# Two 256-column matmuls for one of 512, and 320 bytes of small tiles packed so that operand buffers swap their places modulo 256 bytes

## The chip, the cores and the metric

The kernel runs on one core of one Trainium2 chip. The metric is device time in microseconds (us), from the program's start to its end. The profile used here is one profiled execution on that core: its span, from the first to the last recorded instruction, is 1807.0 us. The timed runs are separate executions. TensorE does the matmuls, VectorE (DVE), ScalarE (ACT) and GpSimd (POOL) the elementwise work, SyncE (SP) issues nearly all transfers.

## What is computed

A trunk of two layers is applied to two groups of 512 tokens with a model width of 1024, in float32. Layer 0 is differential attention, layer 1 a retention in both directions, and a final RMSNorm closes the trunk.

```python
def diff_attention(h, w_in, ...):
    proj = h @ w_in                              # (512, 1024) @ (1024, 8192)
    q, k, v, gate = jnp.split(proj, ...)
    ...                                          # rotary q, k; 8 heads, two softmaxes each
    a = p[:, :, 0] - lam * p[:, :, 1]
    o = einsum('bhqk,bkhe->bqhe', a, v)
    o = rms_norm(o, subln_g, SUBLN_EPS) * (1.0 - lambda_init)
    return (o * silu(gate)) @ w_out              # (512, 2048) @ (2048, 1024)

def bidir_retention(h, w_in, ...):
    proj = h @ w_in                              # (512, 1024) @ (1024, 6144)
    ...                                          # rotated q, k; decayed scores in chunks, both directions
    return (rms_norm(o_f + o_b) * silu(gate)) @ w_out

def trunk(x, ...):
    x = x + diff_attention(rms_norm(x, norm_g[0]), ...)
    x = x + bidir_retention(rms_norm(x, norm_g[1]), ...)
    return rms_norm(x, final_norm_g, NORM_EPS)
```

The two input projections, the two output projections and the attention products are where TensorE's time goes.

## The kernel before

**Precision.** Each float32 operand is split in a high and a low part of the matmul's own float32 format, and a product is the sum of three passes, high by high, high by low and low by high (`PASSES`). ACT writes the high part (`hi_of`, L400), DVE the low one (`lo_of`, L403).

**Projections.** An input projection is cut into units of 256 output columns, and both token groups and both halves of the contraction are combined as in Strassen's scheme in Winograd's form: seven products P1 to P7 per unit instead of eight. The token side of a product is one of seven operands B11, B21, T1, T2, B22, T3, T4, each four tiles of 128 x 2 x 512 (high and low parts), which stay in memory for the whole layer. The weight side is combined, split and put into a ring of seven buffers called `ws`. There are two kinds of units:

- In a *pair* unit (`pair`, L596 to L601: q, k and the gates) the weights are the stationary operand, 128 x 128, and the token operand is the moving one, 512 columns wide. A product is four parts of the contraction by three passes: 12 matmuls into one bank of PSUM. All of them are recorded on L599.
- In a *wide* unit (`wide`, L603 to L612: v) it is the other way round: the token operand is stationary, the weights are the moving one, 256 columns wide, and a product is 48 matmuls into halves of two banks. They are recorded on L609.

Both write the same PSUM ring tiles `pj`, `sc` and `o`. The matmul that opens a bank has `start` set, and where a bank is filled by halves only the first of the two has it.

**The other matmuls.** Attention scores are on L1116 (512 columns), attention times values on L1181 (256), transposes on L1161, L815, L1028 and L716, the retention on L1315, L1339, L1359 and L1367 (256), and the output projection on L891 (512), where the head's output is stationary and the weights in `ws` move.

**Order.** Every operation is given to a planner with a cost and its dependences; `arrange` lays the operations of all five engines out in one simulated order and the kernel issues them in it. A pair product has the cost 2.79 there, whatever it consists of. Instructions of one engine run in the issued order.

**Memory.** Four pools follow each other in every partition of the on-chip memory: `sm` (small tiles of a few elements, each taking 32 bytes), `cp` (large buffers `b`, the identity and tables), `ar` (one tile `arena`, cut into slots of 4 KB that begin 128 bytes in, some of them shifted by 64 or 128 bytes), and `wk` (the rings `ws`, `raw`, `st`, `os`, `c`, `e`, `m`). All large tiles are multiples of 512 bytes, so that the bytes of `sm` and the padding of `arena` set where everything behind them begins modulo 256:

| | large buffers in cp | unshifted slots of the arena | slots shifted by 64 and 128 | rings |
|---|---|---|---|---|
| before | 32 | 32 | 96, 160 | 224 |

The small tiles that the change touches are the column of -0.5 (`mhalf`, 4 elements) and of -1.0 (`minus1`), the twelve one-element tiles of the ring `ssf`, and the two tiles `ls` and `neglam` of the attention's lambda.

Of the kernel before, what the change touches and what calls it, by code (L numbers as in the profile page):

```python
# [19 lines left out]
NT = S // P  # L20
NH = 8
# [5 lines left out]
LAMBDA_INIT = 0.8 - 0.6 * math.exp(-0.3 * 0)  # L27
# [226 lines left out]
def trunk_kernel(  # L254
# [7 lines left out]
    nc = tc.nc  # L262
# [14 lines left out]
    places = {}  # L277
    cnt = [0]

    def view(pool, tag, i, size, shape, dt=F32):  # L280


        if size % 16 and pool in (cp, wk):
            pool = sm
        if (tag, i) not in places:
            places[tag, i] = pool.tile([P, size], F32, tag=f"{tag}{i}", name=f"{tag}_{i}", bufs=1)
        n = math.prod(shape[1:])
        t = places[tag, i][0:shape[0], 0:n]
# [9 lines left out]
        size = SIZE.get(tag, shape[1])  # L298
        return Buf(plan, tag, bufs, lambda i: view(wk, tag, i, size, shape, dt))

    arena = ar.tile([P, 18 * 1024 + 80], F32R, tag="arena", name="arena")

    def slot(n, shape, dt=F32R, shift=0):

# [19 lines left out]
    def const(shape, tag, dt=F32, size=None):  # L324
        return Buf(plan, tag, 1, lambda i: view(cp, tag, i, size or math.prod(shape[1:]), shape, dt))
# [27 lines left out]
    def bank(tag, name=None):  # L353
        return Buf(plan, tag, BUFS[tag], lambda i: view(pj if tag == "pj" else sc, tag, i, S, [P, S]))
# [23 lines left out]
    def pool(n, fn, r, w):  # L378
        plan.op("POOL", 0.15 + 0.0024 * n, fn, r, w)
# [25 lines left out]

    ident = const([P, P], "ident")
    dma(lambda: ident.t, lambda: ident_in, [], [ident], 64, nc.scalar)
    mhalf = const([P, NT], "mhalf")
    dve(4, lambda: nc.vector.memset(mhalf.t, -0.5), [], [mhalf])
    minus1 = const([P, 1], "minus1")  # L410
    dve(1, lambda: nc.vector.memset(minus1.t, -1.0), [], [minus1])
    rows = work("m", [P, P], 4, name="rows")
    gcol = const([P, 28], "gcol")
    dve(1, lambda: nc.vector.memset(gcol[:, 20:21], D * EPS), [], [(gcol, 4)])
# [103 lines left out]
    class Unit:  # L518
# [67 lines left out]
        def product(self, op):  # L586
            which = BANK_OF[op]
            n_banks = 2 if self.wide else 1
            opens = op in OPENS
            if opens:  # L590
                self.banks[which] = [bank(self.tags[which], which) for _ in range(n_banks)]
            a, b = self.ops.pop(op), B_OF[op]
            bt = [Bop[b, k] for k in range(4)]
            reads = [q[1] for q in a] + bt

            def pair(ps, ks=range(4)):  # L596
                for k in ks:
                    for i, (u, v) in enumerate(PASSES):
                        nc.tensor.matmul(  # L599
                            ps.t, a[u][0]()[:, k, :], bt[k][:, v, :], start=(opens and k == 0 and i == 0),  # L600
                            stop=(k == 3 and i == 2), skip_group_check=True)  # L601

            def wide(ps, t):  # L603
                if self.led and op == "P1" and t == 0:
                    for j in range(NT):
                        nc.tensor.transpose(ps[:, j * P:(j + 1) * P], ident.t, ident.t)
                for k in range(4):
                    for i, (u, v) in enumerate(PASSES):
                        nc.tensor.matmul(  # L609
                            ps[:, (t % 2) * 256:(t % 2) * 256 + 256], bt[k][:, v, t * P:(t + 1) * P],  # L610
                            a[u][0]()[:, k, :], start=(opens and t % 2 == 0 and k == 0 and i == 0),
                            stop=(k == 3 and i == 2), skip_group_check=True)  # L612

            if not self.wide:
                ps = self.banks[which][0]
                if op == "P1" and self in first_units[:2]:
                    for k in range(4):
                        pe(0.7, lambda k=k: pair(ps, (k,)), reads[:2] + [bt[k]], [(ps, k)])
                else:
                    pe(2.79, lambda: pair(ps), reads, [ps])  # L620
                return
            for t in range(NT):
                ps = self.banks[which][t // 2]
                led = self.led and op == "P1" and t == 0
                pe(1.87 if led else 1.43, lambda ps=ps, t=t: wide(ps, t), reads + [ident] * led, [ps])
# [185 lines left out]
    def norm_cols(sq, ps, guard):  # L811

        def fn():
            for t in range(2):
                nc.tensor.transpose(ps[:, t * P:(t + 1) * P], sq[:, t * P:(t + 1) * P], ident.t)  # L815
        pe(0.22, fn, [sq, ident], [ps])
        ss, rr = col(2, "css"), col(2, "crr", 9)
        for t in range(2):
            act(P + 120, lambda t=t: nc.scalar.activation(
                ps[:, 256 + t * P:256 + (t + 1) * P], ps[:, t * P:(t + 1) * P], AF.Copy, accum_out=ss[:, t:t + 1]),  # L820
                [(ps, t)], [(ps, 2 + t), (ss, t)])
        guard(ss)
        pool(200, lambda: nc.gpsimd.tensor_tensor(rr.t, ss.t, mhalf[:, 0:2], op=ALU.pow), [ss, mhalf], [rr])
        return rr

    def new_oT(g):
# [94 lines left out]
    def row_norm(g, t):  # L921

        ss, r = halves.pop((g, t)), col(1, "rsf", 4)
        pool(200, lambda: nc.gpsimd.tensor_tensor(r.t, ss.t, mhalf[:, 0:1], op=ALU.pow), [ss, mhalf], [r])
        return r


# [84 lines left out]
    def x_norm(g, t, late=()):  # L1012
        ss, r = col(1, "ssf", 12), col(1, "rsf", 4)
        jk = slot(16 + t % 2, [P, D])
        x = xnat[g, t]
        act(1250, lambda: nc.scalar.activation(jk.t, x.t, AF.Square, accum_out=ss.t), [x, *late], [jk, ss])
        pool(60, lambda: nc.gpsimd.tensor_scalar(ss.t, ss.t, 1.0 / D, EPS, op0=ALU.mult, op1=ALU.add), [ss], [ss])
        pool(200, lambda: nc.gpsimd.tensor_tensor(r.t, ss.t, mhalf[:, 0:1], op=ALU.pow), [ss, mhalf], [r])
        evac(D, lambda: x.t, lambda: x.t, lambda: r.t, [x, r], [x], 0.00058)

    def x_source(layer, tiles, turn):
# [47 lines left out]
    lp = work("m", [P, 2, P], 4, name="lp")  # L1069
    for i in range(2):  # L1070
        dve(P, lambda i=i: nc.vector.tensor_tensor(
            lp[:, i, :], lv.t.rearrange("p a s -> p (a s)")[:, 2 * i * P:(2 * i + 1) * P],
            lv.t.rearrange("p a s -> p (a s)")[:, (2 * i + 1) * P:(2 * i + 2) * P], op=ALU.mult), [lv], [(lp, i)])
    ls, neglam, lr = const([P, 2], "ls"), const([P, 1], "neglam"), const([P, 2, NH], "lr")
    dve(256, lambda: nc.vector.tensor_reduce(ls.t, lp.t, op=ALU.add, axis=AX.X), [lp], [ls])
    act(2, lambda: nc.scalar.activation(ls.t, ls.t, AF.Exp), [ls], [ls])
    dve(2, lambda: nc.vector.tensor_tensor(neglam.t, ls[:, 1:2], ls[:, 0:1], op=ALU.subtract), [ls], [neglam])
    dve(2, lambda: nc.vector.tensor_scalar(neglam.t, neglam.t, -LAMBDA_INIT, None, op0=ALU.add), [neglam], [neglam])
    act(16, lambda: nc.scalar.activation(lr.t, dec.t, AF.Exp), [dec], [lr])
    dve(8, lambda: nc.vector.tensor_scalar(lr[:, 0, :], lr[:, 0, :], -1.0, None, op0=ALU.mult), [lr], [lr])  # L1080
    dma(lambda: powers.t, lambda: dist_in[:, D:].rearrange("p (h t) -> p h t", h=NH), [], [powers], 16)
    for i in range(2):
        dve(16, lambda i=i: nc.vector.tensor_tensor(
            powers[:, :, 2 * i:2 * i + 2], powers[:, :, 2 * i:2 * i + 2], lr[:, i, :].unsqueeze(2).broadcast_to([P, NH, 2]),
            op=ALU.mult), [lr, powers], [powers])
# [52 lines left out]
    def combine(i):  # L1138

        p, sm, n = st[i]['p'], st[i - i % 2]['sm'], i % 2  # L1140
        rc, cc = col(tag="rc"), col(tag="cc")
        on, eng = (pool, nc.gpsimd) if i >= NT else (dve, nc.vector)
        if i >= NT:
            pool(200, lambda: nc.gpsimd.tensor_tensor(rc.t, sm[:, 2 + n:3 + n], minus1.t, op=ALU.pow),
                 [(sm, (1, n)), minus1], [rc])
        else:
            dve(2, lambda: nc.vector.reciprocal(rc.t, sm[:, 2 + n:3 + n]), [(sm, (1, n))], [rc])
        on(100, lambda: eng.tensor_scalar(
            cc.t, sm[:, n:n + 1], rc.t, neglam.t, op0=ALU.mult, op1=ALU.mult), [(sm, (0, n)), rc, neglam], [cc])
# [303 lines left out]
    for i in range(N2 + 1):  # L1453
        if i < N2:
            b, c = chunks[i]
# [78 lines left out]
```

## Time and profile before

| | |
|---|---|
| time of the runs, median of 3 | 1810.51 us (1808.48 to 1814.37) |
| span of the profiled execution | 1807.0 us, 3.5 below that median |
| granted TensorE clock, mean | 0.999 |
| TensorE matmul busy | 1794.9 us, 99% |
| TensorE weight load busy | 1558.1 us, 86% |
| DVE, ACT, POOL busy | 1477.1, 895.1, 169.5 us |
| busy share of the 16 DMA engines in the 40 slices | 0.2 to 0.8 |

PE is the matmul side of TensorE and PEld its weight loads, which run beside the matmuls before them. Matmuls are pipelined: the duration recorded of one contains its way through the array, so that the time a matmul adds is not that duration but the distance from its start to the next one's. That distance is read from rows of the timeline and of the chain of waits that give a start and a count: for a run of n equal matmuls it is the next row's start less this row's, divided by n. In the timeline each row has start, duration, engine, line, operation and tiles; in a list of stretches each row has the stretch, its length, and each engine's busy time with the instructions in it.

### The profile page before, as it was taken

To read this page: it belongs to the slowest core of one execution; us is meant where nothing else is said; L and a number is where in the kernel's file an instruction comes from. 1 tells how busy PE (TensorE), PEld (TensorE's weight loads), DVE (VectorE), ACT (ScalarE), POOL (GpSimd) and SP (SyncE) were. 2 spreads that over 40 slices of the span, in tenths; PEclk is the share of its full clock that TensorE was granted. 3 is DMA by queue.
4 is the path that set the end of the run, shared out by engine and by line. 5 is a ranking of instruction groups with operands and counts; after the bars stand their busy time and mean duration, and the time that the engine had idled before them with its cause. 6 is when DMAs were issued, how large, how long until landed. Compare 5 with 4: busy or idle time off the path is not lost.

```text
span 1807.0 us, 27780 instructions
## 1 busy us (share of the span) xinstructions
PE 1794.9 (99%) x10299; PEld 1558.1 (86%) x10299; DVE 1477.1 (82%) x2319; ACT 895.1 (50%) x1856; POOL 169.5 (9%) x323
## 2 busy tenths in 40 slices
PE   9999999999999999999999999999999999999998
PEld 6789889898988888888888888898989898888887
DVE  7958787778699888888888897787887967888887
ACT  7753444433434565554555866444434355444346
POOL 1000000000000022222322300000000000111113
PEclk9999999999999999999999999999999999999999
DMA  6444455555545685444554524464657559765662
GB/s 217 134 126 137 161 140 178 184 168 155 174 126 175 201 334 198 178 156 159 190 204 140 190 73 146 140 210 146 205 156 228 151 170 396 272 238 182 225 218 94
DMA packets 162767, 328.81 MB, mean 182 GB/s; under 512 B 12724, under 2 KB 76872, under 8 KB 162632
## 3 DMA queue, kind: packets, MB, share of 16 engines
q1 hardware_dynamic: 162304, 326.71, 54.1%
q8 instruction: 81, 1.33, 0.3%
q14 instruction: 54, 0.44, 0.1%
q10 hardware_dynamic: 328, 0.34, 0.1%
HBM read 209.55 MB, written 117.44 MB: 181 GB/s over the span
## 4 chain that ended last, share of the span: by engine, by line
PE 93%; DVE 2%; DMA 2%; ACT 2%; issue 1%; POOL 0%; SPq 0%; POOLq 0%; DVEq 0%; ACTq 0%
PE pj L599 20%; PE pj L891 19%; PE sc L599 10%; PE pj L609 10%; PE o L599 8%; PE o L1181 5%; PE sc L1116 5%; PE sc L609 5%; PE o L609 2%; PE o L1359 2%; PE tp L1161 2%; PE sc L1315 1%; PE o L1367 1%; PE tp L1339 1%; DMA raw<-in_ret_w_out_dram 1%
## 5 line engine op out<-in xcount | busy, mean ns | idle before, releaser
L891 PE MATMUL pj<-ws,arena 128*128 128x512 f32 x1542 | 391.2, 397 | 0.0
L891 PEld LDWEIGHTS pj<-ws,arena 128*128 128x128 f32 x1542 | 277.7, 188 | 52.7
L599 PE MATMUL pj<-b,ws 128*128 128x512 f32 x1080 | 265.0, 392 | 0.0
L599 PEld LDWEIGHTS pj<-b,ws 128*128 128x128 f32 x1080 | 201.4, 188 | 43.0
L403 DVE TENSOR_TENSOR ws<-st,ws 128x512 fp32r<-128x512 f32 (+1 forms) x192 | 147.9, 774 | 74.8 <-ACT ws L400 56.7
L896 DVE SCALAR_TENSOR_TENSOR b<-pj,crr,b 128x512 f32<-128x512 f32 (+1 forms) x257 | 189.9, 744 | 21.4 <-PE pj L891 21.0
L403 DVE TENSOR_TENSOR ws<-raw,ws 128x512 fp32r<-128x512 f32 (+1 forms) x164 | 141.5, 868 | 71.3 <-ACT ws L400 61.0
L400 ACT CAST ws<-st 128x512 fp32r<-128x512 f32 (+1 forms) x192 | 132.4, 693 | 121.4 <-PE pj L599 36.4
L599 PE MATMUL sc<-arena,ws 128*128 128x512 f32 x768 | 186.8, 392 | 0.0
L599 PE MATMUL o<-arena,ws 128*128 128x512 f32 x744 | 180.0, 393 | 1.1 <-ACT m L385 0.6
L599 PEld LDWEIGHTS sc<-arena,ws 128*128 128x128 f32 x768 | 144.0, 188 | 31.3
L400 ACT CAST ws<-raw 128x512 fp32r<-128x512 f32 (+1 forms) x164 | 125.7, 772 | 87.0 <-PE o L599 45.0
L599 PEld LDWEIGHTS o<-arena,ws 128*128 128x128 f32 x744 | 138.4, 188 | 31.7 <-DVE arena L463 1.4
L599 PE MATMUL pj<-arena,ws 128*128 128x512 f32 x648 | 160.3, 392 | 0.4 <-DVE arena L463 0.4
L599 PEld LDWEIGHTS pj<-arena,ws 128*128 128x128 f32 x648 | 120.8, 188 | 26.7 <-DVE arena L463 0.7
L1134 ACT ACTIVATE b<-sc,nm 128x512 f32<-128x512 f32 x128 | 88.0, 689 | 66.9 <-DVE nm L1124 66.5
L636 ACT COPY c<-pj 128x512 f32<-128x512 f32 x104 | 60.9, 586 | 119.7 <-PE pj L599 66.4
L609 PE MATMUL pj<-ws,b 128*128 128x256 f32 x960 | 116.8, 276 | 0.0
L609 PEld LDWEIGHTS pj<-ws,b 128*128 128x128 f32 x960 | 113.2, 188 | 0.7
L1116 PE MATMUL sc<-arena 128*128 128x512 f32 x384 | 101.2, 395 | 0.3 <-ACT b L1134 0.3
L1181 PEld LDWEIGHTS o<-arena 128*128 128x128 f32 x768 | 93.1, 188 | 2.7
L1181 PE MATMUL o<-arena 128*128 128x256 f32 x768 | 93.7, 278 | 0.0
(207 smaller groups left out, 2855.9 us busy)
## 6 DMA issues: line engine op xcount, KB each, us to landing
qk<-os SPq DMA_DIRECT2D x192, 256.0 KB, 3.6
arena<-qk SPq DMA_DIRECT2D x96, 512.0 KB, 5.8
raw<-in_da_w_in_dram SPq DMA_DIRECT2D x64, 512.0 KB, 5.1
v<-os SPq DMA_DIRECT2D x64, 512.0 KB, 4.3
arena<-v SPq DMA_DIRECT2D x64, 512.0 KB, 4.1
raw<-in_ret_w_in_dram SPq DMA_DIRECT2D x48, 512.0 KB, 4.8
os<-g SPq DMA_DIRECT2D x32, 512.0 KB, 7.4
g<-e SPq DMA_DIRECT2D x48, 256.0 KB, 4.6
```

What stands on the lines that cost most here:

```text
L400: act(n, lambda: nc.scalar.copy(dst(), src()), r, w)
L403: dve(n, lambda: nc.vector.tensor_tensor(dst(), src(), hi().bitcast(F32), op=ALU.subtract), r, w)
L599: nc.tensor.matmul(ps.t, a[u][0]()[:, k, :], bt[k][:, v, :], start=(opens and k == 0 and i == 0), stop=(k == 3 and i == 2), skip_group_che ...
L609: nc.tensor.matmul(ps[:, (t % 2) * 256:(t % 2) * 256 + 256], bt[k][:, v, t * P:(t + 1) * P], a[u][0]()[:, k, :], start=(opens and t % 2 == ...
L636: act(S, lambda c=c, ps=ps: nc.scalar.copy(c.t, ps.t), [ps], [c])
L891: nc.tensor.matmul(ps[:, here], o[a][:, e, t * P:(t + 1) * P], u[b][:, e, here], start=(m == 0), stop=(m == 5))
L896: axpy(n, lambda half=half, here=here, ps=ps: nc.vector.scalar_tensor_tensor(half, ps[:, here], rr[:, t % 2:t % 2 + 1], half, op0=ALU.mult ...
L1116: nc.tensor.matmul(s.t, q[:, a, t * P:(t + 1) * P], k[:, b, :], start=(n == 0), stop=(n == 2))
L1134: act(840, lambda j=j, s=s, m=m: nc.scalar.activation(p[:, j, :], s.t, AF.Exp, bias=m.t, accum_out=sm[:, 2 * j + n:2 * j + n + 1]), [s, m] ...
L1161: nc.tensor.transpose(tp[:, j * P:(j + 1) * P], p[:, 0, j * P:(j + 1) * P], ident.t)
L1181: nc.tensor.matmul(o[:, e * 256:(e + 1) * 256], v[b][:, j, e * P:(e + 1) * P], aT[a][:, j, :], start=(n == 0), stop=(n % 12 == 11), skip_g ...
L1359: nc.tensor.matmul(o[:, e * 256:(e + 1) * 256], v_[v][:, 2 * c + j, e * P:(e + 1) * P], a_[:, u, j * 256:(j + 1) * 256], start=(e == 0 and ...
```

## The change

- `pair` issues two matmuls of 256 columns, left half and right half of the bank, with the same stationary operand one after the other, where there was one of 512. `start` is set for the left one of the first pass alone.
- `minus1` becomes a fifth column of `mhalf`, `neglam` a third column of `ls`, and the twelve tiles of `ssf` become columns of one tile of 32. `sm` is 320 bytes shorter by that (twelve times 32 less 128, and twice 32).
- `arena` is 32 elements (128 bytes) longer.

Behind that the buffers begin, modulo 256:

| | large buffers in cp | unshifted slots of the arena | slots shifted by 64 and 128 | rings |
|---|---|---|---|---|
| after | 224 | 224 | 32, 96 | 32 |

On each of the five engines the instructions stand in the same order as before, with two matmuls of 256 in the place of each one of 512 on L599.

```diff
+        if tag == "ssf":
+            if tag not in places:
+                places[tag] = sm.tile([P, 16 + 16], F32, tag=tag, name=tag, bufs=1)
+            return places[tag][:, i:i + 1]
...
-    arena = ar.tile([P, 18 * 1024 + 80], F32R, tag="arena", name="arena")
+    arena = ar.tile([P, 18 * 1024 + 112], F32R, tag="arena", name="arena")
...
-    mhalf = const([P, NT], "mhalf")
-    dve(4, lambda: nc.vector.memset(mhalf.t, -0.5), [], [mhalf])
-    minus1 = const([P, 1], "minus1")
-    dve(1, lambda: nc.vector.memset(minus1.t, -1.0), [], [minus1])
+    mhalf = const([P, NT + 1], "mhalf")
+    dve(4, lambda: nc.vector.memset(mhalf[:, 0:NT], -0.5), [], [(mhalf, 0)])
+    dve(1, lambda: nc.vector.memset(mhalf[:, NT:NT + 1], -1.0), [], [(mhalf, 1)])
...
             def pair(ps, ks=range(4)):
                 for k in ks:
                     for i, (u, v) in enumerate(PASSES):
-                        nc.tensor.matmul(
-                            ps.t, a[u][0]()[:, k, :], bt[k][:, v, :], start=(opens and k == 0 and i == 0),
-                            stop=(k == 3 and i == 2), skip_group_check=True)
+                        for c in range(2):
+                            here = slice(c * 256, (c + 1) * 256)
+                            nc.tensor.matmul(
+                                ps[:, here], a[u][0]()[:, k, :], bt[k][:, v, here],
+                                start=(opens and k == 0 and i == 0 and c == 0),
+                                stop=(k == 3 and i == 2), skip_group_check=True)
...
-    ls, neglam, lr = const([P, 2], "ls"), const([P, 1], "neglam"), const([P, 2, NH], "lr")
+    ls, lr = const([P, 3], "ls"), const([P, 2, NH], "lr")
...
-    dve(2, lambda: nc.vector.tensor_tensor(neglam.t, ls[:, 1:2], ls[:, 0:1], op=ALU.subtract), [ls], [neglam])
-    dve(2, lambda: nc.vector.tensor_scalar(neglam.t, neglam.t, -LAMBDA_INIT, None, op0=ALU.add), [neglam], [neglam])
+    dve(2, lambda: nc.vector.tensor_tensor(ls[:, 2:3], ls[:, 1:2], ls[:, 0:1], op=ALU.subtract), [(ls, 0)], [(ls, 1)])
+    dve(2, lambda: nc.vector.tensor_scalar(ls[:, 2:3], ls[:, 2:3], -LAMBDA_INIT, None, op0=ALU.add),
+        [(ls, 1)], [(ls, 1)])
```

The rest of the diff names the new columns where the old tiles were read.

More of the change, by code (lines that the diff above doesn't have):

```diff
@@ L822, in norm_cols @@
         guard(ss)
-        pool(200, lambda: nc.gpsimd.tensor_tensor(rr.t, ss.t, mhalf[:, 0:2], op=ALU.pow), [ss, mhalf], [rr])
+        pool(200, lambda: nc.gpsimd.tensor_tensor(rr.t, ss.t, mhalf[:, 0:2], op=ALU.pow), [ss, (mhalf, 0)], [rr])
         return rr
@@ L923, in row_norm @@
         ss, r = halves.pop((g, t)), col(1, "rsf", 4)
-        pool(200, lambda: nc.gpsimd.tensor_tensor(r.t, ss.t, mhalf[:, 0:1], op=ALU.pow), [ss, mhalf], [r])
+        pool(200, lambda: nc.gpsimd.tensor_tensor(r.t, ss.t, mhalf[:, 0:1], op=ALU.pow), [ss, (mhalf, 0)], [r])
         return r
@@ L1017, in x_norm @@
         pool(60, lambda: nc.gpsimd.tensor_scalar(ss.t, ss.t, 1.0 / D, EPS, op0=ALU.mult, op1=ALU.add), [ss], [ss])
-        pool(200, lambda: nc.gpsimd.tensor_tensor(r.t, ss.t, mhalf[:, 0:1], op=ALU.pow), [ss, mhalf], [r])
+        pool(200, lambda: nc.gpsimd.tensor_tensor(r.t, ss.t, mhalf[:, 0:1], op=ALU.pow), [ss, (mhalf, 0)], [r])
         evac(D, lambda: x.t, lambda: x.t, lambda: r.t, [x, r], [x], 0.00058)
@@ L1073, in trunk_kernel @@
             lv.t.rearrange("p a s -> p (a s)")[:, (2 * i + 1) * P:(2 * i + 2) * P], op=ALU.mult), [lv], [(lp, i)])
-    ls, neglam, lr = const([P, 2], "ls"), const([P, 1], "neglam"), const([P, 2, NH], "lr")
-    dve(256, lambda: nc.vector.tensor_reduce(ls.t, lp.t, op=ALU.add, axis=AX.X), [lp], [ls])
-    act(2, lambda: nc.scalar.activation(ls.t, ls.t, AF.Exp), [ls], [ls])
-    dve(2, lambda: nc.vector.tensor_tensor(neglam.t, ls[:, 1:2], ls[:, 0:1], op=ALU.subtract), [ls], [neglam])
-    dve(2, lambda: nc.vector.tensor_scalar(neglam.t, neglam.t, -LAMBDA_INIT, None, op0=ALU.add), [neglam], [neglam])
+    ls, lr = const([P, 3], "ls"), const([P, 2, NH], "lr")
+    dve(256, lambda: nc.vector.tensor_reduce(ls[:, 0:2], lp.t, op=ALU.add, axis=AX.X), [lp], [(ls, 0)])
+    act(2, lambda: nc.scalar.activation(ls[:, 0:2], ls[:, 0:2], AF.Exp), [(ls, 0)], [(ls, 0)])
+    dve(2, lambda: nc.vector.tensor_tensor(ls[:, 2:3], ls[:, 1:2], ls[:, 0:1], op=ALU.subtract), [(ls, 0)], [(ls, 1)])
+    dve(2, lambda: nc.vector.tensor_scalar(ls[:, 2:3], ls[:, 2:3], -LAMBDA_INIT, None, op0=ALU.add),
+        [(ls, 1)], [(ls, 1)])
     act(16, lambda: nc.scalar.activation(lr.t, dec.t, AF.Exp), [dec], [lr])
@@ L1143, in combine @@
         if i >= NT:
-            pool(200, lambda: nc.gpsimd.tensor_tensor(rc.t, sm[:, 2 + n:3 + n], minus1.t, op=ALU.pow),
-                 [(sm, (1, n)), minus1], [rc])
+            pool(200, lambda: nc.gpsimd.tensor_tensor(rc.t, sm[:, 2 + n:3 + n], mhalf[:, NT:NT + 1], op=ALU.pow),
+                 [(sm, (1, n)), (mhalf, 1)], [rc])
         else:
@@ L1148, in combine @@
         on(100, lambda: eng.tensor_scalar(
-            cc.t, sm[:, n:n + 1], rc.t, neglam.t, op0=ALU.mult, op1=ALU.mult), [(sm, (0, n)), rc, neglam], [cc])
+            cc.t, sm[:, n:n + 1], rc.t, ls[:, 2:3], op0=ALU.mult, op1=ALU.mult), [(sm, (0, n)), rc, (ls, 1)], [cc])
         axpy(S, lambda: nc.vector.scalar_tensor_tensor(
```

## Prediction

> **What bounds the kernel now.** I read the page's first part, then the chain that ended last, then the timeline of TensorE.
>
> ```profile
> PE 1794.9 (99%) x10299; PEld 1558.1 (86%) x10299; DVE 1477.1 (82%) x2319; ACT 895.1 (50%) x1856; POOL 169.5 (9%) x323
> PEclk9999999999999999999999999999999999999999
> PE 93%; DVE 2%; DMA 2%; ACT 2%; issue 1%; POOL 0%; SPq 0%; POOLq 0%; DVEq 0%; ACTq 0%
> ```
>
> The reader is to see that matmuls cover 99% of the span, at a clock that no slice shows throttled, and that 93% of the chain is matmul. So the time is the number of matmuls times the distance between their starts, and what other engines do counts only if they come to delay a matmul. DVE has 18% in hand over the span, so a PE that is half a per cent faster doesn't run into it.
>
> The change has two edits: one alters the number and width of the matmuls of L599, the other where operands begin. How many matmuls the first reaches:
>
> ```profile
> L599 PE MATMUL pj<-b,ws 128*128 128x512 f32 x1080 | 265.0, 392 | 0.0
> L599 PE MATMUL sc<-arena,ws 128*128 128x512 f32 x768 | 186.8, 392 | 0.0
> L599 PE MATMUL o<-arena,ws 128*128 128x512 f32 x744 | 180.0, 393 | 1.1 <-ACT m L385 0.6 <-DVE arena L463 0.3
> L599 PE MATMUL pj<-arena,ws 128*128 128x512 f32 x648 | 160.3, 392 | 0.4 <-DVE arena L463 0.4
> L599 PE MATMUL sc<-b,ws 128*128 128x512 f32 x120 | 29.1, 391 | 0.0
> ```
>
> That is 3360 matmuls, 280 products of 12.
>
> **What a matmul of either width costs.** The timeline (start, duration, engine, line, operation) and the chain (start, length, count):
>
> ```profile
> 163.42 5.63 PE L609 MATMUL o<-ws,arena 128*128 128x256 f32 x48
> 168.88 5.60 PE L609 MATMUL sc<-ws,arena 128*128 128x256 f32 x48
> 174.32 0.84 PE L609 MATMUL pj<-ws,b 128*128 128x256 f32 x6
> ...
> 190.64 1.54 PE L599 MATMUL pj<-arena,ws 128*128 128x512 f32 x6
> ```
>
> ```profile
> 210.01 8.24 PE pj L599 x36
> 218.25 2.75 PE o L599 x12
> ```
>
> Three pair products take 218.25 - 210.01 = 8.24 us, 2.747 us a product, 228.9 ns for a matmul of 512 columns. Wide units already run 256 columns with a fresh weight load each: 48 take 174.32 - 168.88 = 5.44 us, 113.3 ns each, and the whole stretch of 240 takes 190.64 - 163.42 = 27.22 us, 113.4 ns. Two of these are 226.7 ns. So 256-column matmuls are, in this trace, a little cheaper per column.
>
> **The split, step by step.** It adds 3360 matmuls and 3360 weight loads and leaves the columns the same. What carries the added loads:
>
> ```profile
> 163.42:190.64 27.22, 27.22 (x241) 27.22 (x240) 19.34 (x29) 12.07 (x20) 0.00 (x0) 1.00 0.56 172
> 486.38:626.46 140.08, 140.08 (x615) 114.93 (x614) 125.00 (x201) 59.54 (x105) 0.00 (x0) 1.00 0.50 153
> ```
>
> In a stretch of L609 the weight side is busy for all of the 27.22 us (third figure), in one of L599 for 114.93 of 140.08. The split moves L599 from the second regime to the first: a load no longer hides with room to spare under its matmul, it fills the distance. In the first regime nothing is left over, and yet 240 in a row held 113.4 ns.
>
> A product becomes 24 x 113.3 = 2.720 us instead of 2.747: -0.027 us, times 280 = -7.5 us. The first 48 of a run cost 168.88 - 163.42 = 5.46, 0.02 us more than settled ones; wide and pair units then have the same width, so what pair runs pay at their start, wide runs may save at theirs: I put 0.
>
> There is another spacing of 256-column matmuls, here called the long one, and the upper bound of the price comes from it:
>
> ```profile
> 705.64 1.64 PE L891 MATMUL pj<-ws,arena 128*128 128x512 f32 x6
> 707.12 2.99 PE L1181 MATMUL o<-arena 128*128 128x256 f32 x24
> 709.95 1.56 PE L1116 MATMUL sc<-arena 128*128 128x512 f32 x6
> ...
> 793.64 2.92 PE L1181 MATMUL o<-arena 128*128 128x256 f32 x24
> 796.39 0.60 PE L1161 MATMUL tp<-ident,b 128*128 128x128 f32 x4
> ```
>
> ```profile
> L1315 PE MATMUL sc<-arena 128*128 128x256 f32 x192 | 28.0, 282 | 0.1
> ```
>
> The same 24 matmuls of L1181 take 2.75 us at 793.64 and 2.83 at 707.12, 117.9 ns each. L1315 shows the same spacing as a mean: 282 ns recorded, where L609's rows below have 276 and 277. A pair product at the long spacing costs +0.083 us. So the split is worth between -7.5 and 280 x 0.083 = +23 us. I take -7.5: the nearest row is L609, whose moving and stationary operands begin at 224 and 32 modulo 256, exactly where the changed pair's do.
>
> **The new places.** Every address is still 32 modulo 64; what moves is the stationary operand's place less the moving one's, modulo 256. L599 goes from 224 - 32 = 192 to 32 - 224 = 64, L609 from 64 to 192, L891 (160 and 224 before, 96 and 32 after) from 192 to 64. Matmuls with both operands in the arena and large buffers keep theirs.
>
> - L609, 2688 matmuls, comes to 192. Rows of 256 columns at that relation are L1359 and L1367:
>
> ```profile
> 1560.46 1.52 PE L1359 MATMUL o<-arena 128*128 128x256 f32 x12
> 1561.82 0.84 PE L1367 MATMUL o<-arena,b 128*128 128x256 f32 x6
> 1562.50 1.55 PE L891 MATMUL pj<-ws,arena 128*128 128x512 f32 x6
> L609 PE MATMUL pj<-ws,b 128*128 128x256 f32 x960 | 116.8, 276 | 0.0
> L609 PE MATMUL sc<-ws,arena 128*128 128x256 f32 x768 | 89.6, 276 | 0.0
> L609 PE MATMUL pj<-ws,arena 128*128 128x256 f32 x576 | 73.1, 277 | 0.0
> L609 PE MATMUL o<-ws,arena 128*128 128x256 f32 x384 | 45.0, 277 | 0.0
> ```
>
> 1.36 / 12 and 0.68 / 6 are 113.3 ns too. Taken: 0; at worst all of it at the long spacing, 2688 x 4.6 = +12.4 us; at best the 0.02 at the head of its runs, under 1 us.
>
> - L891, 1530 matmuls, comes to 64, where no 512-column matmul of this trace stands. Its price now, from the chain, and its count:
>
> ```profile
> 1783.58 13.76 PE pj L891 x60
> L891 PE MATMUL pj<-ws,arena 128*128 128x512 f32 x1530 | 389.8, 398 | 0.0
> ```
>
> 13.76 / 60 = 229.3 ns. At twice the settled 256-column price it would gain 2.6 ns, -4.0 us in all; at twice the long one, 235.8, it would lose +9.9. Taken: 0, as L599 and L891 agree to 0.4 ns at the one relation both have.
>
> - L1181 keeps its relation; which spacing it has may be drawn anew. It has 32 products of 24, so at most 32 x 0.08 = 2.6 us either way. Taken: 0.
> - DVE, ACT, POOL and transfers see other addresses, at the same 32 modulo 64. I bound that only by cover: DVE is idle for 18% of the span, transfers fill about half of the 16 engines (0.56 and 0.50 in the stretches above). Taken: 0; if the cover went, DVE would be late with `ws` and L599 or L609 would wait.
> - The packing moves no instruction. `ssf`, -1.0 and lambda are columns now; their readers stand in the same order behind the same producers. It takes no DMA, nor is anything moved past SP's or POOL's queue. 0.
> - The added instructions must be fetched: q8, which carries PE's, moved 1.33 MB for 2 x 10299 of them.
>
> ```profile
> q8 instruction: 81, 1.33, 0.3%
> ```
>
> A third more of 0.3% is hidden, at L609's rate of issue as shown. 0.
>
> **The sum.** 1807.0 - 7.5 = 1799.5 us of span. The median of the runs lies 3.5 above this profile's span, and I add that: 1803.0 us, 0.4% below 1810.51. A kernel of this spread can tell about 0.3% from no change.
>
> **The rivals.**
>
> *The long spacing holds in the pair stream (slower).* Place: weight loads of pair units, now busy all the time. For it: L1181 at 707.12 kept it for all 24, and pair streams give no other width to leave it by. Against it: the 240 of L609. All 280 products so: 1810.5 + 23 = 1834 us. It decides the sign once more than 0.027 / (0.027 + 0.083) = 25% of the products have it. In a milder form each half loses half of the way from 113.3 to 117.9: 2 x 115.6 - 228.9 = +2.3 ns, times 3360 = +7.7 us, 1818 us.
> The Trainium skill speaks against the split in just that size: "TensorE: Matmul & The Clock Gate", in the section asking why the gap is 56 and not 53.3 ns, has a fixed cost of about 2.5 ns per matmul at full clock. By it the added 3360 matmuls would be an estimated +8.4 us, about 1819. The trace doesn't bear it out across these widths, with 226.7 ns for two halves against 228.9 for one whole.
>
> *The new relation slows L891.* The 512-column price is unknown at 64. For it: the long spacing exists at that relation in L1181. Against: that line is 256 wide. With the split's gain, 1803.0 + 9.9 = 1813 us, where the loss outruns the gain once L891 loses 4.9 ns of its possible 6.5.
>
> *The new relation helps L891.* 1803.0 - 4.0 = 1799 us. For it: 512 columns cost more per column than 256 at the old relation. Against it: nothing but the lack of a row.
>
> *The change doesn't do what it says.* If 228.9 ns belong to the pair's operands (stationary ring, moving token operand) and not to the width, the two halves cost what the whole did: 1810.5 us. Against it: L891 has the roles reversed and 229.3.
>
> **How the numbers follow.** The forecast 0.47; L891 helped 0.14; no difference from width 0.05; L891 slowed 0.09; pair partly at the long spacing 0.14; pair wholly 0.11. The forecast's own range is 1799 to 1808, by the 3.5 us of median less span and by L1181's 2.6. Faster by over 0.3% (below 1805.1): the forecast but for 0.06, and L891 helped, 0.41 + 0.14 = 0.55. Within 0.3%: those 0.06, 0.05, and two thirds of L891 slowed, 0.17. Slower: the rest, 0.28. The range from 1796 to 1826 takes in all but a pair stream wholly at the long spacing, and a few in a hundred below, where helped L891 and re-drawn L1181 meet.
>
> **What would show it.** In the changed trace L599 should have 6720 matmuls of 256 columns with a mean recorded duration of 276 to 277 ns, as L609's rows above, and a settled pair product should take 2.72 us on the chain. If its mean is 281 or 282, or a product takes 2.83, the long spacing has won. L609 should stay at 113.3 ns; L891 should keep 13.76 us for 60. PE's share stays 99%, PEld rises to nearly that, and no new group of waits for DVE, ACT or DMA appears ahead of L599. The prediction is wrong if the spacing of the pair stream isn't L609's, or if L891's price depends on the relation by more than 5 ns.

## The result and the profile after

The changed kernel takes 1821.76 us (median of 6 runs, 1818.93 to 1829.03), the kernel before 1808.43 beside it. The ratio is 1.0074, with a 95% interval of 1.0058 to 1.0089: slower by 0.7%, where 1803 was forecast. The profiled execution has a span of 1819.1 us, 12.1 more than before.

The page's first part and the instruction queue:

```profile
PE 1806.4 (99%) x13659; PEld 1706.0 (94%) x13659; DVE 1479.4 (81%) x2319; ACT 896.2 (49%) x1856; POOL 170.3 (9%) x323
PEclk9999999999999999999999999999999999999999
q8 instruction: 107, 1.75, 0.4%
```

TensorE is as dense as before, at the same clock, and the other engines have the same instructions and are busy within 2.5 us of before. So the time came from the distances between matmuls. The groups of matmuls that answer to those of before (busy time, mean recorded ns):

```profile
L897 PE MATMUL pj<-ws,arena 128*128 128x512 f32 x1530 | 393.5, 400 | 0.0
L604 PE MATMUL pj<-b,ws 128*128 128x256 f32 x2160 | 265.5, 278 | 0.0
L604 PE MATMUL sc<-arena,ws 128*128 128x256 f32 x1536 | 187.6, 278 | 0.0
L604 PE MATMUL o<-arena,ws 128*128 128x256 f32 x1488 | 180.0, 278 | 1.1 <-ACT m L389 0.6 <-DVE arena L466 0.5
L604 PE MATMUL pj<-arena,ws 128*128 128x256 f32 x1296 | 161.3, 278 | 0.3 <-DVE arena L466 0.3
L615 PE MATMUL pj<-ws,b 128*128 128x256 f32 x960 | 118.5, 278 | 0.0
L615 PE MATMUL sc<-ws,arena 128*128 128x256 f32 x768 | 90.5, 277 | 0.0
```

L604 is the pair line (L599 before), L615 the wide one (L609), L897 the output projection (L891). No pair group shown is cheaper than before, and those of the wide units and the output projection are dearer: 118.5 for 116.8, 90.5 for 89.6, 393.5 for 389.8. The means of 278 lie between the 276 of the short and the 282 of the long spacing, and the chain shows that they are a mixture (start, length, count):

```profile
247.16 8.16 PE pj L604 x72
...
343.99 8.48 PE pj L604 x72
...
1795.43 14.02 PE pj L897 x60
```

Three pair products take 8.16 us (113.3 ns a matmul) in one stretch and 8.48 (117.8) in another. Sixty matmuls of the output projection take 14.02 us for 13.76.

Adding the distances from start to start of all matmuls of a line, waits among them, gives the account, in us. The last row adds the two retention lines L1359 and L1367 of before, whose stationary operand stands 192 bytes beyond the moving one (modulo 256) in every kernel here:

| | before | after | change |
|---|---|---|---|
| pair units, 3360 x 512 or 6720 x 256 columns | 774.3 | 775.6 | +1.3 |
| wide units, 2688 x 256 | 305.7 | 309.7 | +3.9 |
| output projection, 1530 x 512 | 360.8 | 364.5 | +3.7 |
| attention scores, 384 x 512 | 89.8 | 90.6 | +0.8 |
| retention, 576 x 256 | 66.0 | 68.7 | +2.7 |

These add up to 12.4 us, against 12.1 in the span; the remaining lines gave back 0.3.

**Where the spacing changes.** The changed kernel's timeline of TensorE in two places:

```profile
189.54 2.99 PE L604 MATMUL pj<-arena,ws 128*128 128x256 f32 x24
192.37 5.82 PE L615 MATMUL pj<-ws,b 128*128 128x256 f32 x48
198.03 2.89 PE L604 MATMUL o<-arena,ws 128*128 128x256 f32 x24
200.76 2.88 PE L604 MATMUL sc<-arena,ws 128*128 128x256 f32 x24
203.48 1.52 PE L604 MATMUL pj<-b,ws 128*128 128x256 f32 x12
```

```profile
285.08 2.88 PE L604 MATMUL pj<-b,ws 128*128 128x256 f32 x24
287.80 5.61 PE L615 MATMUL pj<-ws,arena 128*128 128x256 f32 x48
293.24 2.99 PE L604 MATMUL pj<-b,ws 128*128 128x256 f32 x24
296.07 4.17 PE L615 MATMUL o<-ws,arena 128*128 128x256 f32 x34
```

In the first, 24 pair matmuls take 2.83 us, 48 wide ones 5.66 (117.9 ns each), and then pair products 2.73 and 2.72 (113.3). In the second it goes the other way: 2.72, 5.44 (113.3), then 2.83. In this trace each of the 24 boundaries from wide to pair units turns the spacing over, 14 times from long to short and 10 from short to long. The 23 from pair to wide keep it. Where nothing stands between the matmuls it holds for hundreds: over 900 short ones in a row, and 1224 long ones. Transposes between two stretches of the same kind can turn it as well: they did at 10 of the 16 places of L722 in layer 1, and what decides there stays open.

### The profile page after: what moved, and what is told of

The parts are those of the page before. It is cut to its first block, busy times and chain, and to the rows that moved or that the text cites. A ratio compares the mean times of both kernels' runs of the same rounds, so it can differ in the third digit from the quotient of the medians.

```text
span 1819.1 us, 34495 instructions
## 1 busy us (share of the span) xinstructions
PE 1806.4 (99%) x13659; PEld 1706.0 (94%) x13659; DVE 1479.4 (81%) x2319; ACT 896.2 (49%) x1856; POOL 170.3 (9%) x323
## 3 DMA queue, kind: packets, MB, share of 16 engines
q8 instruction: 107, 1.75, 0.4%
## 4 chain that ended last, share of the span: by engine, by line
PE 93%; DVE 2%; DMA 2%; ACT 1%; issue 1%; POOL 0%; SPq 0%; POOLq 0%; DVEq 0%; ACTq 0%
PE pj L604 20%; PE pj L897 19%; PE sc L604 10%; PE pj L615 10%; PE o L604 8%; PE o L1188 5%; PE sc L1123 5%; PE sc L615 5%; PE o L615 2%; PE o L1366 2%; PE tp L1168 2%; PE o L1374 1%; PE sc L1322 1%; PE tp L1346 1%; DMA raw<-in_ret_w_out_dram 1%
## 5 line engine op out<-in xcount | busy, mean ns | idle before, releaser
L897 PE MATMUL pj<-ws,arena 128*128 128x512 f32 x1542 | 394.9, 399 | 0.0
L897 PEld LDWEIGHTS pj<-ws,arena 128*128 128x128 f32 x1542 | 277.8, 188 | 55.2
L604 PE MATMUL pj<-b,ws 128*128 128x256 f32 x2160 | 265.5, 278 | 0.0
L604 PEld LDWEIGHTS pj<-b,ws 128*128 128x128 f32 x2160 | 255.7, 188 | 0.3
L604 PE MATMUL sc<-arena,ws 128*128 128x256 f32 x1536 | 187.6, 278 | 0.0
L604 PEld LDWEIGHTS sc<-arena,ws 128*128 128x128 f32 x1536 | 181.4, 188 | 0.0
L604 PE MATMUL o<-arena,ws 128*128 128x256 f32 x1488 | 180.0, 278 | 1.1 <-ACT m L389 0.6
L604 PEld LDWEIGHTS o<-arena,ws 128*128 128x128 f32 x1488 | 174.5, 188 | 2.1 <-DVE arena L466 1.2
L604 PE MATMUL pj<-arena,ws 128*128 128x256 f32 x1296 | 161.3, 278 | 0.3 <-DVE arena L466 0.3
L604 PEld LDWEIGHTS pj<-arena,ws 128*128 128x128 f32 x1296 | 154.5, 188 | 0.8 <-DVE arena L466 0.5
L615 PE MATMUL pj<-ws,b 128*128 128x256 f32 x960 | 118.5, 278 | 0.0
L615 PEld LDWEIGHTS pj<-ws,b 128*128 128x128 f32 x960 | 114.3, 188 | 0.0
```

Source lines behind the costliest of these rows:

```text
L604: nc.tensor.matmul(ps[:, here], a[u][0]()[:, k, :], bt[k][:, v, here], start=(opens and k == 0 and i == 0 and c == 0), stop=(k == 3 and i ...
L615: nc.tensor.matmul(ps[:, (t % 2) * 256:(t % 2) * 256 + 256], bt[k][:, v, t * P:(t + 1) * P], a[u][0]()[:, k, :], start=(opens and t % 2 == ...
L897: nc.tensor.matmul(ps[:, here], o[a][:, e, t * P:(t + 1) * P], u[b][:, e, here], start=(m == 0), stop=(m == 5))
```

## The experiments

Below, the *difference* is the start of the stationary operand less that of the moving one, modulo 256 bytes. Pair units stand at 192 before and 64 after, wide units at 64 and 192, the output projection at 192 and 64. Sums are formed as in the table above, from the one profiled execution of each kernel.

### Each edit alone

- split only: the kernel before, `pair` with two matmuls of 256 columns
- packing only: the changed kernel, `pair` with one matmul of 512 columns

> The kernel before with pair products in matmuls of 256 columns, all tiles where they were before (large buffers at 32, rings at 224 modulo 256). Theory A (a run of 256-column matmuls keeps its distance, 113.3 or 117.9 ns, until a boundary between wide and pair units turns it over; it has nothing to do with the packing): the projections behave as in the changed kernel, L599 and the wide units together +5 us against before, and L891, L1116, L1359 and L1367 stay as before: 1812 to 1815 us. Theory B (the new places are what makes 256 columns dear, and at the old ones the pair stream settles at 113.3 ns as L1359 does): -7.5 us, 1801 us. Theory C (a fixed cost of about 2.3 ns per added matmul whatever the place): L599 evenly at 115.4 ns, wide units at 113.4, 1810 to 1816 us, and no matmul run at 117.9.

> The changed kernel with pair products in matmuls of 512 columns again: the new places alone. Theory A: pair runs of 512 put the wide units back at 113.5 ns, which gives 4 us; the output projection (L891 of before) stays at 233 ns instead of 230.4 without waits (+3.7 us), and the 256-column lines of the retention behind it stay at 117.8 (+2.7). If 512-column pair matmuls take the same 2.5 ns at their new relation as the output projection does, +8 us more: 1823 us; if they stay at 229.0, 1815 us. Theory B (the split did all the harm): 1808 us, as before.

The split alone took 1826.04 us, 1.0098 [1.0083, 1.0113] of before, and the packing alone 1840.00, 1.0174 [1.0157, 1.0191]. Either alone costs more than both together.

| | pair | wide | output projection |
|---|---|---|---|
| before | 774.3 | 305.7 | 360.8 |
| split only | 790.6 | 309.9 | 360.8 |
| packing only | 787.7 | 317.0 | 364.5 |
| both | 775.6 | 309.7 | 364.5 |

The profiled execution of the split alone took 1829.37 us, 3.3 more than the median of its four runs.

The chain of the packing alone:

```profile
75.61 8.40 PE pj L602 x36
...
157.24 5.66 PE pj L612 x48
...
1814.40 14.02 PE pj L894 x60
```

Pair matmuls of 512 columns at the new places take 8.40 / 36 = 233.3 ns for 228.9, and the wide ones behind them 117.9 for 113.3 throughout. So the new places make 512 columns dear, the split takes most of that back, and at the old places, where 512 columns are cheap, the split only brings the long spacing in. The split alone has it over most of the pair stream:

```profile
272.99 8.16 PE pj L601 x72
...
350.14 8.48 PE pj L601 x72
505.51 8.48 PE pj L601 x72
525.29 8.48 PE pj L601 x72
```

Here the boundary that turns the spacing is the other one. From pair to wide units 19 of 23 turn it; the other four are wide runs of 12 matmuls ahead of transposes, in which it stayed long. From wide to pair all 24 keep it. For the split alone theory A had 1812 to 1815 and was too low, as it took the changed kernel's share of long stretches for this one. It also held that the places have nothing to do with it, and they decide which boundary turns the spacing. For the packing alone it had at most 1823 us, as pair runs of 512 columns were to put the wide units back at 113.5 ns. They came out at 117.9, and the kernel at 1840. Theory B fell. Theory C, an even cost per added matmul, fell with the rows: no settled stretch lies at 115.4 ns.

### One matmul left whole

```diff
-                        for c in range(2):
+                        parts = 1 if whole and k == 0 and i == 0 else 2
+                        for c in range(parts):
```

`whole` is true for a pair product that follows a wide one.

> The changed kernel with one matmul left whole, 512 columns, at the head of every pair product that follows a wide one. Theory A (a 512-column matmul sets the spacing back to the short one, as at the head of the wide runs of before): pair and wide runs all at 113.3 ns, no stretch at 117.9; pair -13 us and wide -4 us against the changed kernel, 1804 to 1807 us. Theory B (the places make it): as the changed kernel, 1821. Theory C (a fixed cost): as the changed kernel, 1821.

> The split with the whole matmul at the head of pair products that follow wide ones, at the old places. Theory A: all projections at 113.3 ns and every other line as before: -7.5 us against before, 1800 to 1802 us. Theory B: as the split alone. Theory C: 1814 us.

On the changed kernel: 1813.98 us, 1.0024 [1.0014, 1.0034] of before, 8 less than the changed kernel, where theory A had 15 to 18. Two rows of its chain:

```profile
135.94 8.48 PE pj L610 x72
214.81 8.16 PE pj L610 x72
```

The stretches ahead of the first wide run stay long (8.48), and from 214.81 on the longest pair rows of the chain are all 8.16. Of the 24 boundaries from wide to pair 18 went from short to short and 5 from long to short; one stayed long, and none turned to long. The wide units, whose places and neighbours in the code are those of the changed kernel, came down from 309.7 to 307.0. Pair units gave 1.0 only (774.6): 1439 of their matmuls were still long, two thirds of them in the first 167 us, where the changed kernel has 2064, and longer waits near the start took back a part.

At the old places the same edit did the opposite: 1841.33 us, 1.0172 [1.0155, 1.0188], pair 796.0, wide 317.0, long at all 24 boundaries. A single 512-column matmul doesn't always set the spacing back, so theory A fell in that form. What stood after these four runs: an undisturbed run of 256-column matmuls has one of two spacings, and keeps it.

### The difference or the place

| rings at | pair in columns of | arena, elements |
|---|---|---|
| 160 | 512 | 18 * 1024 + 80 |
| 96 | 512 | 18 * 1024 + 64 |
| 224 | 512 | 18 * 1024 + 96 |
| 160 | 256 | 18 * 1024 + 80 |

All four are the changed kernel, large buffers at 224, with another length of the arena, and three of them have the pair in 512 columns again.

> Pair products in 512 columns, large buffers at 224 as in the changed kernel, the arena 128 bytes shorter, so that rings begin at 160: every operand stands 64 bytes lower modulo 256 than in the kernel before, and every difference between stationary and moving operand is that of before (192 for pair units and the output projection, 64 for wide ones). Theory R (the difference modulo 256 sets the distance of 512-column matmuls): pair 229.0 ns, output projection 230.4 without waits, wide 113.5, 1806 to 1811 us as before. Theory P (the places themselves do, 32 and 224): anything else, up to the 1840 us of the packing alone.

> Pair products in 512 columns, large buffers at 224, rings at 96: pair and wide units at a difference of 128, the output projection at 0. Theory R: the pair shows one price for 128 and the output projection one for 0, and the next kernel shows the same two prices with the roles exchanged. Theory P: no such exchange. No row tells the level; between 226 and 236 ns for 512 columns.

> Pair products in 512 columns, large buffers and rings both at 224: pair and wide units at a difference of 0, the output projection at 128. Theory R: the two prices of the kernel with 128 and 0, exchanged. Theory P: no exchange.

> The places of the kernel with rings at 160 and large buffers at 224, and pair products in 256 columns. Theory R (the difference also says at which boundary a 256-column run changes its distance): as the split alone at the old places, a turn from 113.3 to 117.9 or back at every boundary from pair to wide units, none from wide to pair, 1826 us. Theory P (the turn comes where the one moving operand and the next stationary one both begin at 32): no boundary has that, no turns, and all projections at one distance: 1801 us at 113.3 or 1845 at 117.9.

The first has other places than the kernel before and the same differences. It took 1808.96 us, 1.0002 [0.9991, 1.0012], and each sum agrees with before to 0.1 us (774.3, 305.7, 360.8). Two rows of its chain:

```profile
75.02 8.24 PE pj L602 x36
...
1783.26 13.76 PE pj L894 x60
```

Its split form took 1826.53, 1.0099 [1.0079, 1.0119], as the split alone, and its boundaries turn the spacing where that kernel's do, in 20 of the 23 from pair to wide and in none from wide to pair. Theory P fell on both. The packing itself, smaller tiles and columns, costs nothing.

The chains of the two others, at 128 and at 0 for the pair:

```profile
75.40 8.37 PE pj L602 x36
...
1812.51 13.64 PE pj L894 x60
```

```profile
74.90 8.16 PE pj L602 x36
...
168.47 5.76 PE sc L612 x48
...
1800.38 13.97 PE pj L894 x60
```

With the pair at 128 and the output projection at 0 (first fence) they take 8.37 / 36 = 232.5 and 13.64 / 60 = 227.3 ns. With the roles exchanged (second) the pair at 0 takes 226.7 and the output projection at 128 takes 232.8. The price goes with the difference, not with the line, as theory R had it. In time they are 1838.37 us, 1.0164 [1.0144, 1.0185], and 1826.64, 1.0099 [1.0079, 1.0120]: the second has the cheapest pair of all, 768.6 us, and loses it in the wide units, 322.8 us at 120 ns (5.76 / 48).

### The remaining differences

Rings at 192, 128, 0 and 64, by an arena of 18 * 1024 + 88, + 72, + 104 and + 120 elements, with the pair in 512 columns.

> Pair products in 512 columns, large buffers at 224, rings at 192: pair units at a difference of 224, wide ones at 32, the output projection at 160. Theory R: settled 512-column matmuls of the output projection take what the pair takes in the kernel with a difference of 160, and the other way round. If the price follows a smooth course between the four places seen (0: 226.7, 64: 233.3, 128: 232.5, 192: 228.9 ns), the pair is near 227.8 and the output projection near 230.7: pair -3.7 us, wide unknown between 113.3 and 120 ns (0 to +18 us). Rival: these starts are whole multiples of 64 and the old ones are not, and the price goes by that: all lines off the course.

> Rings at 128: pair units at a difference of 160, wide ones at 96, the output projection at 224. Theory R: the two prices of the kernel with 224 and 160, exchanged; on a smooth course pair near 230.7 (+6 us) and output projection near 227.8.

> Rings at 0: pair units at a difference of 32, wide ones at 224, the output projection at 96. On a smooth course pair near 230 (+3.7 us), output projection near 232.9 (+6).

> Rings at 64: pair units at a difference of 96, wide ones at 160, the output projection at 32. Theory R: the two prices of the kernel before this one, exchanged; on a smooth course pair near 232.9 (+13 us), output projection near 230.

They took 1842.79, 1840.27, 1839.68 and 1847.13 us, ratios 1.0188, 1.0174, 1.0171 and 1.0212, none with an interval that reaches below 1.014. The price in ns of a 512-column matmul by difference, from the chain rows of 36 pair and 60 output matmuls:

| difference | 0 | 32 | 64 | 96 | 128 | 160 | 192 | 224 |
|---|---|---|---|---|---|---|---|---|
| pair | 226.7 | 233.3 | 233.3 | 234.2 | 232.5 | 233.3 | 228.9 | 233.3 |
| output projection | 227.3 | 233.5 | 233.7 | 234.5 | 232.8 | 233.7 | 229.3 | 233.5 |

The two rows come from different kernels but for 64 and 192, and agree to 0.6 ns. The wide units add to the times: at the differences 32, 96, 224 and 160 they sum up to 318.5, 317.7, 314.1 and 322.7 us. The smooth course that I expected isn't there: 0 and 192 are two low places, and the rest lies between 232.5 and 234.5. Whether the four odd multiples of 32 are dear for their difference or because these rings begin at whole multiples of 64 can't be told apart here.

### One line's operand alone

So far all lines moved at once. Here the pair weights alone are written 64 bytes further on in buffers that are 256 bytes longer, in the kernel before, so that the pair stands at 0, the wide units at 64 and the output projection at 192. The ring `e` has seven tiles for eight, and a control has that without the 64 bytes.

```diff
-    SIZE = dict(ws=1024, ...)
+    SIZE = dict(ws=1088, ...)
-        return work("e", [P, S], 8, name=name)
+        return work("e", [P, S], 7, name=name)
-                s = ws_t([P, 2, 4, n])
+                s = ws_t([P, 2, 4, n], 16)      # the control: 0
```

> The kernel before, in 512 columns, with the pair weights alone written 64 bytes further on in their buffers (which are 256 bytes longer; the ring e has seven tiles instead of eight to make room): pair units stand at a difference of 0, wide ones stay at 64 and the output projection at 192. Theory R (each line's own difference sets its price): pair settles at 226.7 ns (768.6 us for its 3360 matmuls instead of 774.3), everything else as in its control: 5.7 us less than the control with the same ring of seven. Theory S (a 256-column run takes the spacing that the 512-column run before it left, whatever its own difference): wide runs come out at 117.8 ns or more behind pairs at 0, +11 us, and the whole is 5 us slower than the control.

> The control: the kernel before with the longer weight buffers and seven tiles of e, no weights moved. Every difference between operands as before; both theories say pair 229.0 and wide 113.5 ns, as before; what the smaller ring costs in waits is in its time alone, 1808 to 1815 us.

The control took 1809.19 us, 1.0002 [0.9994, 1.0011]; the kernel with the pair at 0 took 1813.24, 1.0019 [1.0010, 1.0028]. The chain of the latter, then of the control:

```profile
74.63 8.16 PE pj L599 x36
...
162.37 5.65 PE o L609 x48
...
1788.19 13.76 PE pj L891 x60
```

```profile
76.86 8.24 PE pj L599 x36
...
195.38 5.47 PE pj L609 x48
...
1785.40 13.76 PE pj L891 x60
```

The pair gains what its own difference says, as theory R had it: 768.4 us, against 774.3 in the kernel before and 776.1 in the control. But theory R left everything else as in the control, 5.7 us less, and the kernel takes 4 us more; theory S had 5 more. The wide units haven't moved, are still at 64, and go from 305.9 us to 316.4, 117.7 ns each on average. What changed is what runs ahead of them.

The retention lines say the same over all kernels. Their own difference is 192 everywhere, and the output projection runs ahead of nearly all their runs. L1359's 384 matmuls add up to 43.6 to 43.7 us in each kernel whose output projection stands at 192, and to 45.0 to 45.3 in each of the others. The attention scores, at 192 everywhere too, add up to 89.8 us in the former and to 90.1 to 90.6 in the latter.

The last run leaves the pair at 0 except for the last product ahead of each wide one, which stays at 192.

```diff
-                s = ws_t([P, 2, 4, n], 16)
+                s = ws_t([P, 2, 4, n], 0 if last else 16)
```

> The kernel with pair weights 64 bytes further on (pair units at a difference of 0), but with the last pair product ahead of every wide one left at 192, as in the kernel before. Theory S (a 256-column run takes the spacing that the 512-column run before it left; one at 192 leaves 113.3 ns, one at 0 leaves 117.8): wide runs back at 113.4 to 113.7 ns, 305.7 us, pair at 226.7 but for 24 products of 12 at 229.0, 769.0 us: 5 us below the kernel before, 1803 to 1804 us. Rival (the twelve are too few, or the whole stretch behind decides): wide runs stay at 117.8, 1813 us.

It took 1808.53 us, 0.9998 [0.9989, 1.0007]: as before, not 5 us below. The pair sums up to 770.9 us and the wide units to 311.7, where 769.0 and 305.7 were expected. Its chain in layer 0 and in layer 1:

```profile
163.51 5.65 PE o L609 x48
169.16 5.65 PE sc L609 x48
...
1180.87 5.47 PE o L609 x48
1186.34 5.44 PE sc L609 x48
```

In layer 0 the wide runs stay long (5.65), in layer 1 they are short but for two runs of 36 matmuls, with the same twelve matmuls at 192 ahead of them. So the last product doesn't decide alone. Nor does a difference alone set the price of so short a run of 512 columns, as the timeline shows at two places of layer 1:

```profile
1275.36 2.96 PE L599 MATMUL pj<-b,ws 128*128 128x512 f32 x12
1278.16 5.62 PE L609 MATMUL o<-ws,arena 128*128 128x256 f32 x48
1283.62 0.62 PE L609 MATMUL sc<-ws,arena 128*128 128x256 f32 x4
...
1305.38 2.91 PE L599 MATMUL pj<-arena,ws 128*128 128x512 f32 x12
1308.13 5.63 PE L609 MATMUL pj<-ws,b 128*128 128x256 f32 x48
1313.60 1.76 PE L599 MATMUL o<-arena,ws 128*128 128x512 f32 x7
```

Both products stand at 192. The first follows a long wide run and takes 2.80 us, 233.3 ns a matmul, the price of 32, 64, 160 and 224; the second follows a short one and takes 2.75, 229.2 ns. The wide runs behind both are short, 5.46 and 5.47 us for 48. What a whole stretch hands on from its beginning, over 512-column matmuls too, stays open. So does the reason why one kind of boundary turns the spacing, and whether the dear differences have a price of their own or only keep a run at a dear spacing that it would leave at 192. No version beat the kernel before.

## Why the prediction was wrong

**The split's price.** The step "A product becomes 24 x 113.3 = 2.720 us instead of 2.747" took the settled spacing of the wide units for the pair's, and it is the step that failed. The rows it rests on were right (113.3, 113.4, 117.9 ns), and so was the count: 6720 matmuls. But a short spacing isn't a property of the width or of the wide units' own places: with nothing moved but the pair weights, those units went to 117.7 ns. They were short behind 512-column pair runs at 192, and the change took those runs away. Measured: 775.6 us for 774.3, where -7.5 was forecast. The rival of a pair stream partly at the long spacing, 1818 us with 0.14, comes nearest; its break-even of 25% long products was passed, with 31% of the pair matmuls long (2064 of 6720). By its two prices that share makes about +2 us, and +1.3 was measured. Why it was 31% and not, as in the split alone, some 80%, is known only as far as the boundaries go; which spacing a stream starts with stays open.

**The wide units.** "Taken: 0" failed, by +3.9 us within the bound of 12.4. They have the spacing that the pair stream hands them. L1359 and L1367 were no evidence for it: their 113.3 ns comes and goes with the difference of the output projection ahead of them.

**The output projection.** "Taken: 0, as L599 and L891 agree to 0.4 ns at the one relation both have" failed: two lines at one difference can't tell what another costs. 233.7 for 229.3 ns in the settled rows, and +3.7 us in the sum, within the bound of +9.9. Settled rows alone would make it 1530 x 4.4 = 6.7; most of this line runs in groups of 6 and 12 between other matmuls. The rival that the new relation slows it was right in kind, and was in force together with the long spacing, which the cases had as alternatives.

**Lines that keep their difference.** The bound for re-drawn spacing covered L1181 alone, which didn't move (88.4 and 88.3 us). The retention's +2.7 us, on L1359 and L1367, and the scores' +0.8 had no term at all, as lines that keep their difference were taken to keep their price.

**The packing and the cover.** Instructions fetched (1.75 MB), waits, DVE, ACT and transfers were rightly put at 0: no new wait stands ahead of a pair matmul, and the kernel with the packing and the old differences runs as before.

**The split and the packing together.** I summed them as independent terms. They aren't: +17.5 us and +31.5 alone, +13.3 together.

**The offset.** The 3.5 us added for the median less the span came from three runs. Over six the kernel before has 1808.43 us, 1.4 above that span, so this term was 2 us too large. It doesn't touch the sign.

**The Trainium skill's fixed cost** ("TensorE: Matmul & The Clock Gate", the section on 56 and 53.3 ns) gave 1819 by its estimate, nearest to the time of all figures, and not by what happens here. Settled halves lie at 113.3 or 117.8 ns. That makes a split worth -2.3 or +6.7 ns against the 228.9 of the old places, and -6.7 or +2.3 against the 233.3 of the new ones. An even +2.5 per added matmul isn't there: at the old places the split added 16.3 us to the pair's sum, at the new ones it took 12.1 away.

## What to carry to other kernels

A distance read from a settled run belongs to that run's neighbours too: before it is used as the price of another stream, ask what stood ahead of the run, and whether the change removes it. Where TensorE is dense, look at where its two operands begin relative to each other before changing widths, and change one thing at a time: a sweep of one padding constant showed 2% (1808.96 to 1847.13 us) between the best and the worst place, and two edits that each cost time made a smaller loss together.

## What the runs showed of the hardware

- The distance of float32 matmuls of 512 columns, each with its own 128 x 128 weight load, depends in settled runs on where the stationary operand begins relative to the moving one modulo 256 bytes: 226.7 to 227.3 ns at 0, 228.9 to 229.3 at 192, 232.5 to 234.5 at the six other multiples of 32. At two places twelve matmuls at 192 right behind a long run took 233.3.
- The Trainium skill ("SBUF — State Buffer", the section on who interferes with whom) gives TensorE two read ports, one for the moving operand and one for weight loads, and calls them independent. It doesn't lead one to expect that the two starts matter relative to each other, and the measurement decides. A resource shared behind the ports would explain it; no run here shows one.
- Matmuls of 256 columns have two stable spacings, 113.3 and 117.8 ns at the differences 64 and 192, for the same instructions at the same places. With the pair split, one lasts in an undisturbed stream until a boundary between kinds of unit turns it over: from wide to pair where the pair stands at 64, from pair to wide (39 of 46 in two kernels) where it stands at 192. Transposes can turn it too. Behind pair runs of 512 columns, wide units at the other differences took 116.7 ns (224) to 120 (0 and 160).
- The changed kernel's six runs spread over 10 us, the four of the packing alone, which has no turns, over 2 (1839.85 to 1841.80), and the six of the kernel before over 6. That the share of long stretches varies between executions would fit, but only one execution of each kernel was profiled.
